# Turning the weights of mLSTM head 0 by transfers in place of TensorE, and issuing the row broadcasts of heads 1 and 2 ahead of their stores

## The chip, the cores and the metric

The kernel runs on one core of one Trainium2 chip. The metric is the device time of one execution in microseconds. The core has a matrix engine (TensorE, PE in the profile), a vector engine (VectorE, DVE), an activation engine (ScalarE, ACT), a general engine (GpSimd, POOL), a queue engine (SyncE, SP) and a set of DMA engines that move data between the core's memories and DRAM. Each engine works through its own list of instructions in order.

## The reference, cut to what matters

The model has two layers with 256 context and 256 latent tokens of width 1024. Layer 0 mixes tokens by a bidirectional mLSTM with four heads, layer 1 by latent attention; a gated convolution FFN follows each. The change touches the mLSTM alone:

```python
def step(carry, inp):                       # one chunk of one head, one direction
    ...
    b = jnp.cumsum(fc, axis=-1)
    dmat = jnp.where(tril, b[..., :, None] - b[..., None, :] + ic[..., None, :], -jnp.inf)
    ...
    wmat = jnp.exp(dmat - mj[..., None]) * jnp.einsum("bhjd,bhsd->bhjs", qc, kc)
    ...
    num = g[..., None] * jnp.einsum("bhjd,bhde->bhje", qc, C) + jnp.einsum("bhjs,bhse->bhje", wmat, vc)
    den = g * jnp.einsum("bhjd,bhd->bhj", qc, n) + jnp.sum(wmat, -1)
    h = num / jnp.maximum(jnp.abs(den), jnp.exp(-mj))[..., None]
...
hsum = o * s.transpose(0, 2, 1, 3)          # o: sigmoid output gate, s: both directions added
return _head_rms_norm(hsum, norm_g) @ w_out
```

## The kernel before

The kernel doesn't scan chunks. For each head it forms the whole 512 x 512 matrix of weights, row blocks `t` of 128 query tokens against column blocks `s` of 128 key tokens. Rows 0 and 1 (context) see columns 0 and 1; rows 2 and 3 (latent) see all four, so there are 12 blocks of 128 x 128. A block's weight is the exponential of gate sums times the scores `S`, divided by its row's normaliser and added up over the two directions. All products keep float32 accuracy by splitting an operand in a rounded high part and a low remainder (`split`: a cast on ACT, a subtraction on DVE) and multiplying three times (`mm3`, lines 447, 450 and 451).

**The stages.** `build` runs the heads in a loop. In turn h it computes the products `qk` of head h (`w_qk`: 4 outputs, each from 2 weight tiles, each tile 24 products of 128 x 512), then `av` of head h-1 (weights times values), then the scores `s_mm` of head h. Between the tiles `tick` steps background generators, two steps after each tile of `qk`. In turn 1 the generator is `head(0, S)`. In turns 2 and 3 it is `mixed(head(h-1), post)`, which steps the weights of one head and the normalisation of the head before by a plan, a string in which `h` is a step of `head`, `p` one of `post`, `L` a load that turns and `S` a split.

**The weights of a head** (`head`). Two rows of gate sums are broadcast from DRAM over 128 partitions (`aB`, line 1073, issued on POOL), masks are added (`Am`, line 1078, DVE), and three groups follow: exponentials on ACT (line 1115), products with `S` on DVE (1116), normalisers (1122 to 1126), scaling and adding of the directions (1131, 1133). The result is `P[t]`, with queries in the partitions. `av` needs keys in the partitions, so 12 turns of 128 x 128 on TensorE follow (line 1147) into three banks `PT`, each of which is split (461, 462). `av` uses `PT` as the operand that is loaded (`LDWEIGHTS`) against `v`.

**Turning by transfers** exists already for other data: `post` copies a head's output as two planes of 16-bit halves (`planes`, line 466, tile `pl`), stores the planes to DRAM (`hd`, line 1228, POOL), and `turn_load` fetches them with a transposing DMA from ACT's queue (line 1269, tile `hx`); `turn_split` splits them.

**Buffers and order.** Weight tiles `raw` are loaded by SP, cast on ACT (line 361) and reduced on DVE (384) into one of three buffers `w` (`NB`); a cast waits until PE has released the buffer. `s2` is a ring of 15 tiles of 128 x 512 that `aB`, `Am`, `W`, `S`, `pl`, `hx`, `vr` and `oh` share. `v_load` fetches the values `vr` and the output gates `oh` of a head on POOL. Beside this, background work of the modulation (`junk` and `adav`, lines 566 and 581) runs on DVE and ACT. A scheduler puts the instructions of each engine in order from the order of the code and the dependences.

Of the kernel before, what the change touches and what calls it, by code (L numbers as in the profile page):

```python
# [10 lines left out]
U16 = mybir.dt.uint16  # L11
# [23 lines left out]
NB, NRAW, NU, NS = 3, 3, 31, 15  # L35
# [381 lines left out]
class K:  # L417
# [651 lines left out]
    def head(self, h, S, big=False):  # L1069
        nc, last = self.nc, big  # L1070
        aB = [self.s2("aB0"), self.s2("aB1")]
        for d in range(2):
            nc.gpsimd.dma_start(aB[d], self.ad[d, h:h + 1, :].to_broadcast([128, 512]))
        if not big:
            self.t4_step(2)
        Am = [self.s2("Am0"), self.s2("Am1")]
        for d in range(2):
            nc.vector.tensor_tensor(Am[d].rearrange("p (t s) -> p t s", t=4),
                                    aB[d].rearrange("p (t s) -> p t s", t=4),
                                    self.mask[:, d:d + 1, :].to_broadcast([128, 4, 128]), op=ALU.add)  # L1080
        yield
        full = {0: [(0, 0), (0, 128), (0, 256), (0, 384)], 1: [(128, 256), (0, 0), (0, 256), (0, 256)]}
        P = []
        for g in range(3):
            jbs = [0, 1] if g == 0 else [g + 1]
            if big:
                w = self.uf("W")
                W = [w[:, 0:512], w[:, 512:1024]]
            else:
                W = [self.s2("W0"), self.s2("W1")]  # L1090
            den = self.tiny(4, "den")
            nd = len(jbs)
            rng = {}
            for i, t in enumerate(jbs):
                base = 256 * i if g == 0 else 0
                for d in range(2):
                    o = W[d]
                    bias = self.gcol[:, 0, t, 32 * d + h:32 * d + h + 1]
                    spans = [(t * 128, (t + 1) * 128, Am[d])]
                    if d == 0:  # L1100
                        if t > 0:
                            spans.append((0, t * 128, aB[d]))
                        lo, hi = 0, (t + 1) * 128
                    else:
                        if t == 0:
                            spans.append((128, 256, aB[d]))
                        if t >= 2:
                            spans.append((0, 256, aB[d]))
                        if t == 2:
                            spans.append((384, 512, aB[d]))  # L1110
                        lo, hi = {0: (0, 256), 1: (128, 256), 2: (0, 512), 3: (0, 512)}[t]
                    if d == 1 and t == 3:
                        nc.vector.memset(o[:, 256:384], 0.0)
                    for s0, s1, src in spans:
                        nc.scalar.activation(o[:, base + s0:base + s1], src[:, s0:s1], AF.Exp, bias=bias, scale=1.0)
                    nc.vector.scalar_tensor_tensor(o[:, base + lo:base + hi], o[:, base + lo:base + hi], 1.0,
                                                   S[g][:, base + lo:base + hi], op0=ALU.mult, op1=ALU.mult,
                                                   accum_out=den[:, 2 * i + d:2 * i + d + 1])
                    rng[i, d] = (base + lo, base + hi)
            dv = den[:, 0:2 * nd]  # L1120
            R = self.tiny(4, "R")
            nc.vector.scalar_tensor_tensor(R[:, 0:2 * nd], dv, -1.0, dv, op0=ALU.mult, op1=ALU.max)
            e = self.gcol[:, 1, jbs[0]:jbs[-1] + 1, h::32]
            nc.vector.tensor_tensor(R[:, 0:2 * nd].rearrange("p (t d) -> p t d", d=2),
                                    R[:, 0:2 * nd].rearrange("p (t d) -> p t d", d=2), e, op=ALU.max)
            nc.vector.reciprocal(R[:, 0:2 * nd], R[:, 0:2 * nd])
            for i, t in enumerate(jbs):
                big = {0: 1, 1: 0, 2: 1, 3: 0}[t]
                b0, b1 = rng[i, big]
                s0, s1 = rng[i, 1 - big]  # L1130
                nc.vector.tensor_scalar(W[big][:, b0:b1], W[big][:, b0:b1], R[:, 2 * i + big:2 * i + big + 1], None,
                                        op0=ALU.mult)
                nc.vector.scalar_tensor_tensor(W[big][:, s0:s1], W[1 - big][:, s0:s1],
                                               R[:, 2 * i + 1 - big:2 * i + 2 - big], W[big][:, s0:s1],
                                               op0=ALU.mult, op1=ALU.add)
                P.append((W[big], b0))
            yield
        for _ in range(5 if last else 1):
            yield
        self.PT = []  # L1140
        for grp in ([(t, s) for s in range(2) for t in (0, 1)], [(t, s) for s in range(2) for t in (2, 3)],
                    [(t, s) for s in (2, 3) for t in (2, 3)]):
            pt = self.ps("PT")
            lead = None
            for n, (t, s) in sorted(enumerate(grp), key=lambda x: -x[1][0] * (x[1][0] > 1)):
                src, b0 = P[t]
                q = nc.tensor.transpose(pt[:, n * 128:(n + 1) * 128], src[:, b0 + s * 128:b0 + (s + 1) * 128], self.ident)
                if lead is None:
                    lead = q
                elif t > 1:  # L1150
                    self.behind(q, [lead])
            u = self.u("PT")
            self.split(u[:, 0], u[:, 1], pt)
            self.PT.append(u)
        yield

    def v_load(self, h):
# [34 lines left out]
    def av(self, h):  # L1192
        nc = self.nc
        PT, v = self.PT, self.vh
        ts = []
        for t in range(4):
            ps = self.ps("av")
            if t < 2:
                blocks = [(PT[0], s, s) for s in range(2)]
            else:  # L1200
                blocks = [(PT[1], s, s) for s in range(2)] + [(PT[2], s, s + 2) for s in range(2)]
            for n, (u, i, s) in enumerate(blocks):
                c = slice(i * 256 + (t % 2) * 128, i * 256 + (t % 2) * 128 + 128)
                self.mm3(ps, (u[:, 0, c], u[:, 1, c]), (v[s][:, 0], v[s][:, 1]), n == 0, n == len(blocks) - 1)
            ts.append(ps)
        for t in range(4):
            nc.vector.tensor_tensor(self.oh[t], ts[t], self.oh[t], op=ALU.mult)
        r = self.oh
        self.PT = self.vh = self.oh = None
        return r  # L1210
# [36 lines left out]

    def mixed(self, head, post):

        plan = "p hp h hL h hL . L hS LS h S S . . ."  # L1250
        for step in plan.split():
            for op in step:
                if op in "hp":
                    next(head if op == "h" else post, None)
                elif op == "L":
                    self.turn_load()
                elif op == "S":
                    self.turn_split()
            yield
# [1289 lines left out]
```

## Time and profile before

| | us |
|---|---|
| median of 3 timed runs | 1339.59 (1339.39 to 1340.36) |
| the profiled execution, its own time | 1341.12 |
| its span, first to last instruction | 1339.1 |
| granted TensorE clock, mean | 0.999 |
| products `qk` of head 1, in which head 0's weights are made | 401.6 to 446.5 |
| twelve turns of head 0 | 417.9 to 421.4 |
| twelve turns of head 1, of head 2 | about 486, about 543 |

The prediction quotes rows of several views. A row of a timeline reads: start, duration, engine, line, operation, output<-inputs, partitions x elements, and in brackets the idle time before it with what ended it. A row of a group has the smallest, the median and the largest duration in ns. A row of waits names who waited, for whom, and the total, the number and the longest.

### The profile page before, as it was taken

How to read it: one execution, taken by the hardware profiler on the slowest of the kernel's cores; microseconds unless marked ns; L12 is line 12 of the kernel's file. 1: busy time of each engine (PE TensorE's matmuls, PEld its weight loads, DVE VectorE, ACT ScalarE, POOL GpSimd, SP SyncE). 2: the span in 40 equal slices, each digit the busy share in tenths (PEclk: the TensorE clock that was granted, in tenths of full speed). 3: DMA queues.
4: the chain of work that ended last, by engine and by line, in shares of the span. 5: the costliest groups of instructions: out<-in, count | busy, mean ns of one | idle time of the engine just before them, and what ended most of it. 6: DMA issues, size and time to landing. Idle time of an engine off the chain costs nothing.

```text
span 1339.1 us, 18750 instructions
## 1 busy us (share of the span) xinstructions
PE 1326.7 (99%) x6573; PEld 1111.3 (83%) x6573; DVE 1077.2 (80%) x1783; ACT 729.9 (55%) x1271; POOL 165.3 (12%) x268
## 2 busy tenths in 40 slices
PE   8999999999999999999999999999999999999997
PEld 5777888888888888888898888888888988988876
DVE  4798957678688596987979978768899889899996
ACT  4765544445734555574643334333567768567772
POOL 0212000011110111120002011111000022020100
PEclk9999999999999999999999999999999999999999
DMA  9988947889685486875628989967967597497791
GB/s 366 324 276 290 333 161 252 243 270 313 235 262 190 156 245 200 295 276 209 228 75 276 322 264 283 280 177 180 321 223 221 175 243 222 165 303 233 250 336 49
DMA packets 116990, 325.52 MB, mean 243 GB/s; under 512 B 21416, under 2 KB 40360, under 8 KB 116624
## 3 DMA queue, kind: packets, MB, share of 16 engines
q1 hardware_dynamic: 64288, 223.37, 48.6%
q0 software_dynamic: 33360, 81.43, 22.7%
q10 hardware_dynamic: 19248, 19.54, 4.5%
q8 instruction: 51, 0.84, 0.2%
q14 instruction: 43, 0.35, 0.1%
HBM read 289.51 MB, written 56.80 MB: 259 GB/s over the span
## 4 chain that ended last, share of the span: by engine, by line
PE 98%; DVE 1%; DMA 0%; issue 0%; ACT 0%; SPq 0%; DVEq 0%; ACTq 0%
PE fin L1573 8%; PE y L450 6%; PE y L451 6%; PE y L447 6%; PE tok L447 6%; PE tok L450 6%; PE tok L451 6%; PE fin L447 6%; PE fin L451 6%; PE fin L450 6%; PE qk L447 4%; PE qk L451 4%; PE qk L450 4%; PE up L746 2%; PE up L447 2%; PE up L450 1%
## 5 line engine op out<-in xcount | busy, mean ns | idle before, releaser
L361 ACT CAST w<-raw 128x1024 fp32r<-128x1024 f32 (+2 forms) x290 | 300.0, 1037 | 263.6 <-PE tok L451 74.1
L384 DVE TENSOR_TENSOR w<-raw,w 128x1024 fp32r<-128x1024 f32 (+2 forms) x290 | 347.7, 1202 | 114.5 <-ACT w L361 111.0
L566 DVE SCALAR_TENSOR_TENSOR junk<-ar,bc 128x1024 f32<-128x1024 f32 x128 | 155.8, 1218 | 5.1 <-ACT bc L608 2.2
L450 PE MATMUL fin<-h,w 128*128 128x512 f32 (+1 forms) x370 | 139.6, 377 | 0.0
L447 PE MATMUL fin<-h,w 128*128 128x512 f32 (+1 forms) x370 | 139.5, 377 | 0.0
L451 PE MATMUL fin<-h,w 128*128 128x512 f32 (+1 forms) x370 | 139.3, 377 | 0.0
L1573 PE MATMUL fin<-h,w 128*128 128x512 f32 (+1 forms) x636 | 111.1, 337 | 0.0
L1573 PEld LDWEIGHTS fin<-h,w 128*128 128x128 f32 x636 | 97.6, 190 | 13.2
L447 PE MATMUL qk<-xc,w 128*128 128x512 f32 x256 | 100.1, 391 | 0.0
L451 PE MATMUL qk<-xc,w 128*128 128x512 f32 x256 | 99.7, 389 | 0.0
L450 PE MATMUL qk<-xc,w 128*128 128x512 f32 x256 | 99.6, 389 | 0.0
L450 PEld LDWEIGHTS fin<-h,w 128*128 128x128 f32 x370 | 69.6, 188 | 13.0
L451 PEld LDWEIGHTS fin<-h,w 128*128 128x128 f32 x370 | 69.6, 188 | 12.9
L447 PEld LDWEIGHTS fin<-h,w 128*128 128x128 f32 x370 | 69.6, 188 | 12.6
L451 PEld LDWEIGHTS qk<-xc,w 128*128 128x128 f32 x256 | 48.0, 188 | 10.0
L447 PEld LDWEIGHTS qk<-xc,w 128*128 128x128 f32 x256 | 48.1, 188 | 9.9
L450 PEld LDWEIGHTS qk<-xc,w 128*128 128x128 f32 x256 | 48.1, 188 | 9.9
L384 DVE TENSOR_TENSOR wu<-raw,wu 128x1024 fp32r<-128x1024 f32 (+1 forms) x42 | 49.6, 1205 | 4.7 <-ACT wu L361 4.3
L447 PE MATMUL tok<-w,hT 128*128 128x512 f32 x128 | 49.9, 390 | 0.0
L450 PE MATMUL tok<-w,hT 128*128 128x512 f32 x128 | 49.8, 389 | 0.0
L451 PE MATMUL tok<-w,hT 128*128 128x512 f32 x128 | 49.8, 389 | 0.0
L763 ACT ACTIVATE fg<-fg 128x512 f32<-128x512 f32 (+1 forms) x44 | 23.1, 525 | 47.6 <-DVE fg L761 41.2
(520 smaller groups left out, 3146.4 us busy)
## 6 DMA issues: line engine op xcount, KB each, us to landing
raw<-in_ws SPq DMA_DIRECT2D x279, 512.0 KB, 5.3
ar<-in_adaT SPq DMA_DIRECT2D x80, 512.0 KB, 5.7
t4d<-in_ws POOLq DMA_DIRECT2D x20, 512.0 KB, 8.6
zd<-in_ws POOLq DMA_DIRECT2D x18, 512.0 KB, 11.3
adaw<-in_ada SPq DMA_DIRECT2D x16, 512.0 KB, 7.9
raw<-zd SPq DMA_DIRECT2D x12, 512.0 KB, 5.2
zr<-fd ACTq DMA_DIRECT2D x33, 128.0 KB, 4.9
xmd<-xr POOLq DMA_DIRECT2D x16, 256.0 KB, 4.6
```

Source lines behind the costliest of these rows:

```text
L361: self.cast = k.nc.scalar.copy(h[:, :cols], src)
L384: i = self.k.nc.vector.tensor_sub(l[:, :n], src, h[:, :n])
L447: q = mm(out, w[0], x[0], start=start, stop=False, skip_group_check=on)
L450: mm(out, w[0], x[1], start=False, stop=False, skip_group_check=on)
L451: mm(out, w[1], x[0], start=False, stop=stop, skip_group_check=on)
L566: nc.vector.scalar_tensor_tensor(o, w, 1.0, self.bc[j], op0=ALU.mult, op1=ALU.mult, accum_out=col[:, k, j:j + 1])
L746: nc.tensor.matmul(ps[m], wk[i][:, c], hT[k][:, j], start=made[m] == 0, stop=made[m] == 23)
L763: nc.scalar.activation(tmp[:, :n], tmp[:, :n], AF.Silu)
L1573: self.nc.tensor.matmul(ps[:, 0:256] if x else ps, w[x][:, k * 128:(k + 1) * 128], h[:, 0:256] if x else h, start=i == 0 and not k0, stop= ...
```

## The change

Three things change.

1. `head_turn` is new. For head 0 `head` hands `P` to it in place of the twelve turns on TensorE. It copies the four row blocks as 16-bit planes on ACT (three tiles `pl`: rows 0 and 1 share one), stores them by six DMAs on POOL into two DRAM tensors (`wa`: 512 rows by 256 key columns; `wb`: rows 256 to 511 by the other 256), fetches each column block by a transposing DMA from ACT's queue into `wx` (two of 128 x 1024 halves, two of 128 x 512 into one tile), and splits the three tiles `wx` into `PT`. The `yield`s in it spread this over steps 5 to 16 of the stage's sixteen.
2. `PT` becomes a table by block, so that `av` finds a block in either layout. The products of `av` are the same.
3. In heads 1 and 2 `head` yields once after its two broadcasts `aB`, and the plan of `mixed` begins with `hp hp` in place of `p hp`: the broadcasts are issued ahead of the planes and stores of `post`.

```diff
         for d in range(2):
             nc.gpsimd.dma_start(aB[d], self.ad[d, h:h + 1, :].to_broadcast([128, 512]))
+        if h and not big:
+            yield
         if not big:
             self.t4_step(2)
...
             yield
+        if h == 0:
+            yield from self.head_turn(P)
+            return
         for _ in range(5 if last else 1):
             yield
...
+    def head_turn(self, P):
+        nc = self.nc
+        da = self.dr.tile([512, 2, 256], U16, name="wa")
+        db = self.dr.tile([256, 2, 256], U16, name="wb")
+        for g, wait in enumerate((1, 3, 1)):
+            for _ in range(wait):
+                yield
+            pl = self.pool.tile([128, 2, 512], U16, tag="s2", name="pl", bufs=NS)
+            for t, c in ((0, slice(0, 256)), (1, slice(256, 512))) if g == 0 else ((g + 1, slice(0, 512)),):
+                self.planes(pl[:, :, c], P[t][0][:, c])
+            for i in range(2):
+                c = slice(i * 256, (i + 1) * 256)
+                t = i if g == 0 else g + 1
+                d = db[(g - 1) * 128:g * 128] if g and i else da[t * 128:(t + 1) * 128]
+                nc.gpsimd.dma_start(d, pl[:, :, c])
+        yield
+        xs = []
+        for s in range(4):
+            if s % 2 == 0:
+                yield
+            d, n = (da, 512) if s < 2 else (db, 256)
+            if s != 3:
+                x = self.s2("wx")
+                xs.append(x)
+            o = x[:, 256:512] if s == 3 else x[:, 0:n]
+            nc.scalar.dma_start_transpose(o.bitcast(U16), d.rearrange("t h n -> (t h) n")[:, s % 2 * 128:s % 2 * 128 + 128])
+        self.PT = {}
+        for i, x in enumerate(xs):
+            yield
+            u = self.u("PT")
+            self.split(u[:, 0], u[:, 1], x)
...
-        plan = "p hp h hL h hL . L hS LS h S S . . ."
+        plan = "hp hp h hL h hL . L hS LS h S S . . ."
```

**On PE**, in the products `qk` of head 1 (`W` are the weights of row block 2 or 3, `xc` and `w` the operands of `qk`), the second group of turns stood like this before:

```order
L450 MATMUL qk<-xc,w 128x512
L451 MATMUL qk<-xc,w 128x512
L1147 MATMUL PT<-ident,W 128x128 x2
L1147 MATMUL PT<-ident,W_3531 128x128 x2
L1147 MATMUL PT<-ident,W 128x128 x2
L1147 MATMUL PT<-ident,W_3531 128x128 x2
L447 MATMUL qk<-xc,w 128x512
```

and now nothing stands between the products:

```order
L450 MATMUL qk<-xc,w 128x512
L451 MATMUL qk<-xc,w 128x512
L447 MATMUL qk<-xc,w 128x512
L450 MATMUL qk<-xc,w 128x512
L451 MATMUL qk<-xc,w 128x512
```

The first group, four turns of rows 0 and 1 nine products earlier, is gone in the same way. Beside these twelve turns PE's order is what it was, to the end of the program.

**On ACT**, at the same place, from the cast of `w` at which the turned banks were read, before:

```order
L361 CAST w<-raw 128x1024
L461 CAST PT<-PT 128x512
L581 COPY adav<-w 1x1
L461 CAST PT<-PT 128x512 x2
L461 CAST qk<-qk 128x512
L361 CAST w<-raw 128x1024
L581 COPY adav<-w 1x1 x2
L361 CAST w<-raw 128x1024
L581 COPY adav<-w 1x1
L461 CAST qk<-qk 128x512
L461 CAST v<-vr 128x512 x4
L361 CAST w<-raw 128x1024
```

and now, from the copy of the last plane (the other copies stand ahead of it):

```order
L466 COPY pl<-W 128x1024
L461 CAST qk<-qk 128x512
L361 CAST w<-raw 128x1024
L1190 DMA_TRANSPOSE wx<-wa 128x1024 x2
L581 COPY adav<-w 1x1 x2
L361 CAST w<-raw 128x1024
L581 COPY adav<-w 1x1
L1190 DMA_TRANSPOSE wx<-wb 128x512 x2
L461 CAST qk<-qk 128x512
L461 CAST v<-vr 128x512 x4
L361 CAST w<-raw 128x1024
L461 CAST PT<-wx 128x512 x3
```

The transfers stand ahead of the next two casts of `w` and wait there for the stores; the casts of `PT` moved behind a third.

**On POOL**, whose list is its queue of DMAs, from head 0's loads to the stores of its turned output (`t4d` are loads of FFN weights), before:

```order
L1740 DMA t4d<-in_ws 16x8192 x2
L1162 DMA vr<-vd 128x512 x4
L1168 DMA oh<-od 128x512 x4
L1228 DMA hd<-pl 128x1024 x2
L1073 DMA aB_3975<-ad 128x512
L1228 DMA hd<-pl 128x1024 x2
L1073 DMA aB_3976<-ad 128x512
```

and now:

```order
L1781 DMA t4d<-in_ws 16x8192 x2
L1179 DMA wa<-pl 256x1x256 x3
L1179 DMA wb<-pl 256x1x256
L1179 DMA wa<-pl 256x1x256
L1179 DMA wb<-pl 256x1x256
L1206 DMA vr<-vd 128x512 x4
L1212 DMA oh<-od 128x512 x4
L1073 DMA aB_3969<-ad 128x512
L1073 DMA aB_3970<-ad 128x512
L1269 DMA hd<-pl 128x1024 x4
```

Six stores stand ahead of the loads of `v`, and the broadcasts of head 1 stand ahead of the stores `hd`. The same happens to the broadcasts of head 2.

More of the change, by code (lines that the diff above doesn't have):

```diff
@@ L1137, in head @@
             yield
+        if h == 0:
+            yield from self.head_turn(P)
+            return
         for _ in range(5 if last else 1):
             yield
-        self.PT = []
+        self.PT = {}
         for grp in ([(t, s) for s in range(2) for t in (0, 1)], [(t, s) for s in range(2) for t in (2, 3)],
@@ L1153, in head @@
             self.split(u[:, 0], u[:, 1], pt)
-            self.PT.append(u)
+            for n, x in enumerate(grp):
+                self.PT[x] = u, slice(n * 128, (n + 1) * 128)
+        yield
[25 more added lines that the diff above has]
+            nc.scalar.dma_start_transpose(o.bitcast(U16), d.rearrange("t h n -> (t h) n")[:, s % 2 * 128:s % 2 * 128 + 128])
+        self.PT = {}
+        for i, x in enumerate(xs):
+            yield
+            u = self.u("PT")
+            self.split(u[:, 0], u[:, 1], x)
+            for t, s in [(t, i) for t in range(4)] if i < 2 else [(t, s) for s in (2, 3) for t in (2, 3)]:
+                c = t * 128 if i < 2 else (s - 2) * 256 + (t - 2) * 128
+                self.PT[t, s] = u, slice(c, c + 128)
         yield
@@ L1197, in av @@
             ps = self.ps("av")
[L1198 to L1204, printed above, removed]
+            n = 2 if t < 2 else 4
+            for s in range(n):
+                u, c = PT[t, s]
+                self.mm3(ps, (u[:, 0, c], u[:, 1, c]), (v[s][:, 0], v[s][:, 1]), s == 0, s == n - 1)
             ts.append(ps)
```

## The prediction

> **What bounds the kernel now.** I read the busy times first, then the chain that ended last, then what TensorE waited for, then the windows around the changed place.
>
> ```profile
> PE 1326.7 (99%) x6573; PEld 1111.3 (83%) x6573; DVE 1077.2 (80%) x1783; ACT 729.9 (55%) x1271; POOL 165.3 (12%) x268
> ...
> PE 98%; DVE 1%; DMA 0%; issue 0%; ACT 0%; SPq 0%; DVEq 0%; ACTq 0%
> ```
>
> TensorE (PE) is busy for 1326.7 of 1339.1 us, and 98% of the chain that ended last is its work. Only what shortens PE's own row, or leaves PE waiting, can move the end. All that PE waits for in the execution stands in five rows (engine and line, then what it waited for: total us, times, longest):
>
> ```profile
> PE idle L683 <- DVE adav L519: 1.5, 1, 1.5
> PE adar L531 <- DMA adaw<-in_ada: 1.5, 1, 1.5
> PE y L447 <- ACT u L1797: 0.5, 1, 0.5
> PE y L450 <- DVE w L384: 0.3, 1, 0.3
> PE up L746 <- DVE hT L721: 0.3, 1, 0.3
> ```
>
> That is 4.1 us, at the start and in the last FFN product, none of it near the change. The change lies in the products `qk` of heads 1 to 3; their windows (stretch; us in it; busy us and instructions of PE, PEld, DVE, ACT, POOL; clock; DMA share; GB/s):
>
> ```profile
> 400.00:420.00 20.00, 20.00 (x93) 16.54 (x92) 18.50 (x51) 11.29 (x27) 2.68 (x5) 1.00 0.56 184
> 420.00:440.00 20.00, 20.00 (x94) 16.67 (x93) 14.72 (x27) 8.04 (x16) 0.00 (x0) 1.00 0.49 146
> 440.00:460.00 20.00, 20.00 (x96) 16.78 (x95) 13.57 (x23) 9.54 (x20) 0.00 (x0) 1.00 0.49 158
> 460.00:480.00 20.00, 20.00 (x90) 16.57 (x89) 11.66 (x35) 13.70 (x28) 6.94 (x13) 1.00 0.82 216
> 480.00:500.00 20.00, 20.00 (x96) 16.70 (x95) 19.77 (x34) 11.88 (x23) 1.60 (x3) 1.00 0.84 284
> ```
>
> PE is busy for 20.00 of 20.00 us in each, at full granted clock. The first three windows hold head 0's weights, which the change turns in another way. The last two hold head 1, where four such transfers run already for other tiles, with a DMA share of 0.82 to 0.84, and PE loses nothing.
>
> **The change, part by part.**
>
> *Removed from PE: twelve turns.* Around them PE's timeline reads (start, us, engine, line):
>
> ```profile
> 417.68 0.39 PE L451 MATMUL qk<-xc,w 128*128 128x512 f32 x1
> 417.90 0.60 PE L1147 MATMUL PT<-ident,W 128*128 128x128 f32 x4
> 418.26 0.48 PE L447 MATMUL qk<-xc,w 128*128 128x512 f32 x1
> 418.58 0.39 PE L450 MATMUL qk<-xc,w 128*128 128x512 f32 x1
> ...
> 420.19 0.39 PE L451 MATMUL qk<-xc,w 128*128 128x512 f32 x1
> 420.42 1.03 PE L1147 MATMUL PT<-ident,W 128*128 128x128 f32 x8
> 421.21 0.48 PE L447 MATMUL qk<-xc,w 128*128 128x512 f32 x1
> 421.52 0.40 PE L450 MATMUL qk<-xc,w 128*128 128x512 f32 x1
> ```
>
> Undisturbed, a `qk` product starts every 0.227 us: from 421.52 to the first product of `av` at 446.47 (row below) stand 110 of them in 24.95 us. From L451 at 417.68 to L450 at 418.58, two slots on, are 0.90 us in place of 0.45, so four turns cost 0.45. From 420.19 to 421.52 are 1.33, so eight cost 0.88. Sum **1.33 us, 0.11 each**. The chain has the same:
>
> ```profile
> 418.07 0.44 PE PT L1147 x4
> ...
> 420.58 0.87 PE PT L1147 x8
> ```
>
> That is 1.31. I take 1.32. Every other PE instruction keeps its place, so this is the whole direct gain. The turns' own duration is longer:
>
> ```profile
> L1147 PE MATMUL PT<-ident,W x48: 270/272/273, 417.9 to 591.7; 128*128 128x128 f32 x48
> ```
>
> The 272 ns overlap with the neighbours, so they bound the gain from above: 12 x 0.272 = 3.26 us. From below it is bounded by nothing gained. The page "VectorE: DVE Perf Modes" of the Trainium skill, section "The three transpose paths", gives 390 ns for a 128x128 bf16 turn on TensorE and 1309 ns for one by DMA, and its rules for kernel authors prefer TensorE where PSUM will do, which speaks against this change. By that figure the twelve would be 4.7 us (an estimate from the page) and the time 1334.9; the trace's 0.11 us of pitch decides against it.
>
> *Added: planes, stores, transfers, splits.* The rows that price them are those of head 1's turned planes (`pl`, `hd`, `hx`), in the order copy on ACT, store's issue on POOL, its landing (the issues' view from 455 to 512 us), the transfer's issue on ACT's queue, its landing, and the landings of all eight stores:
>
> ```profile
> L466 ACT COPY pl<-oh x8: 1038/1048/1052, 459.5 to 520.6; 128x1024 uint16<-128x1024 uint16 x8
> L1228 POOL DMA_DIRECT2D hd<-pl x8: 539/542/547, 460.8 to 521.9; - x8
> ...
> hd<-pl POOLq DMA_DIRECT2D x4, 256.0 KB, 3.1
> oh<-od POOLq DMA_DIRECT2D x4, 256.0 KB, 8.5
> ...
> L1269 ACTq DMA_TRANSPOSE hx<-hd x8: 1174/1208/1496, 471.7 to 534.4; - x8
> DMA to landing us min/median/max: 3.4/3.6/4.4
> ...
> DMA to landing us min/median/max: 2.3/3.1/4.2
> ```
>
> ACT gets copies of three full planes, 3 x 1.05 = 3.1 us, and four transfer issues of at most 1.2 each. It is idle for about half of the windows above, so nothing of this is on the path by itself; uncovered it would cost 3.1 us plus up to 4.8 of issue. DVE gets no new instruction: the three subtractions of `PT` move. What can reach PE is lateness, so I follow the last plane (row block t=3):
>
> ```profile
> 419.04 0.75 DVE L1133 SCALAR_TENSOR_TENSOR W<-W,R 128x512 f32<-128x512 f32 x1
> ...
> 425.39 1.05 ACT L361 CAST w<-raw 128x1024 fp32r<-128x1024 f32 x1
> ...
> 430.35 1.05 ACT L361 CAST w<-raw 128x1024 fp32r<-128x1024 f32 x1 [3.59 <-PE qk L451]
> ...
> 436.27 2.18 ACT L461 CAST v<-vr 128x512 fp32r<-128x512 f32 x4
> ...
> 437.01 2.49 DVE L462 TENSOR_TENSOR v<-vr,v 128x512 fp32r<-128x512 f32 x4
> ...
> 446.47 0.39 PE L447 MATMUL av<-v,PT 128*128 128x512 f32 x1
> ```
>
> Its weights are done at 419.8, the copy at 420.9, its two stores are issued by 422.0 and land at 425.1 (3.1 each; the stores' 512-byte pieces have no row of their own, so I bound their landing by 2.3, the shortest store, and 8.5, the slowest load in that stretch, and take 3.1 as the nearest in kind). PE-paced times after 421 come 1.32 earlier: the cast of `w` at 425.39 ends at 425.1, then two transfers are issued until 427.5 and land at 431.1. The next cast of `w` ends at 430.1, the two half transfers are out by 432.5 and land by 436.1 (436.9 at 4.4). The casts of `v` end at 437.1, one more `w` at 438.1, and three `PT` casts at 0.55 each (2.18/4) end at 439.8, all data being there. On DVE `v` ends at 438.2, `w` about 439.4, three subtractions of 0.62 (2.49/4) at 441.2. PE wants the first of them at 446.47 - 1.32 = 445.15. **3.9 us to spare**, so cost nothing.
>
> *The new wait, and what stands behind it.* A tile of `w` is cast on ACT and its remainder is taken on DVE:
>
> ```profile
> L384 DVE TENSOR_TENSOR w<-raw,w 128x1024 fp32r<-128x1024 f32 (+2 forms) x290 | 347.7, 1202 | 114.5 <-ACT w L361 111.0
> ```
>
> The transfers wait in ACT's order for the stores. Behind them stands the cast of `w` that was at 430.35, then `qk`, `v`, `w`. That cast waited for PE to release one of three `w` buffers; PE then still has two tiles of 24 x 0.227 = 5.44 us, so it wants the new one 10.9 us after 429.0, at 439.9, and it is ready at 429.0 + 1.05 + 1.2 = 431.3. The cover is 8.6 us. With 2.4 of issue behind it, the stores may land as late as about 435, 13 us after their issue, before PE waits. On POOL the loads `vr` of `v` move behind the six stores: issued by 422.0 + 4 x 0.54 = 424.2, and even at 8.5 us they land at 432.7, ahead of 436.27 - 1.32 = 434.95. The loads `oh` follow by 426.3 and are needed after `av`, past 446.
>
> *Moved: the broadcasts `aB` of heads 1 and 2 ahead of the stores `hd`.* This takes away waits of DVE:
>
> ```profile
> DVE Am L1078 <- DMA aB<-ad: 15.2, 4, 6.0
> ```
>
> At most 15.2 us in four places, 6.0 at one. PE was at 20.00 of 20.00 while DVE stood, so it is worth nothing. Two POOL issues of 0.54 us stand ahead of the stores now, and the buffers of `aB` were last read by splits done before the stores are due: 1.1 us later at worst, and head 1's transfers stand behind ACT work that begins sooner. Also nothing.
>
> **Sum.** The profiled execution's span is 1339.1, its own time 1341.12, so 2.0 lie around the span. The span becomes 1337.8 and that execution 1339.8. It was 1.5 above the median of the three timed runs (1339.59; 1339.39 to 1340.36), so against the median: 1339.59 - 1.32 = **1338.3 us**. That is 0.10%, below the 0.2% (2.7 us) that a measurement of this kernel can tell from no change.
>
> **Rivals.**
> - *Given back.* If PE, being early, waits later for something that it doesn't pace, the gain goes. For it: ACT waits for loads in the next stage (row below). Against it: PE has no wait in 400 to 1270 us at all. Time 1339.6.
>
> ```profile
> ACT wu L361 <- DMA raw<-in_ws: 4.4, 3, 2.7
> ```
>
> - *The whole duration counts.* If a turn held the array for its 272 ns, 3.26 us go: 1336.3. Against it: the pitch above, read at two places. The page "TensorE: Matmul & The Clock Gate", section "Part 4: PE-mode transpose", has about 275 ns in one kernel and says that turns don't count as activity for the clock; the granted clock of 1.00 in these windows shows nothing of that.
> - *Slower: ACT stands at the transfers.* If the stores land later than 435, the cast of `w` is late and PE stands one us for each us. To be slower by 0.2% it takes 1.32 + 2.7 = 4.0 us of standing, so landings near 439, 17 us after issue, as against 3.1 and 8.5 in the rows. Six stores, eight loads and three transfers' worth of data in the same 15 us could do it if the small pieces go badly. At 5 us of standing: 1343.3.
> - *The change doesn't do what it says.* The order of PE without the twelve rows rules this out.
>
> **Chances.** Forecast 74%, given back 12%, ACT held 8%, whole duration 6%. The range reaches from the forecast less the spread of the runs before (0.97): 1337.3, a little wider 1337.2, to "given back" with the highest run's 0.77 above its median: 1340.4. The other two cases, 14%, lie outside. Faster by over 0.2%: 6%. Within: 74 + 12 = 86%. Slower: 8%.
>
> **What would show it.** Right: twelve fewer `PT` rows on PE; PE at 20.00 of 20.00 from 400 to 480; `av` of head 0 starting near 445.15 with no wait; `wx` landed before its casts; DVE's wait for `aB` in heads 1 and 2 gone and the end unmoved by it. Wrong: a wait of PE for `w` near 440 or for `PT` at `av` (ACT held); the same `av` start but an end that isn't earlier (given back); `av` near 443 (whole duration).

## The result, and the profile after

| | before | after |
|---|---|---|
| median of 20 executions each, us | 1340.01 (1339.39 to 1340.85) | 1343.05 (1337.99 to 1348.07) |
| ratio, with its 95% interval | | 1.0019 (1.0010 to 1.0028) |
| profiled execution: its own time, span | 1341.12, 1339.1 | 1339.69, 1337.9 |

The changed kernel's executions fall in two groups: nine from 1337.99 to 1340.58, median 1339.38, and eleven from 1342.74 to 1348.07. Before, all 20 lie within 1.5 us. (The ratios here and below are taken over all executions; the quotient of the two medians is 1.0023.) The profile is of an execution of the first group and shows on PE what was forecast. The page's busy times, and the windows (columns as in the prediction):

```profile
PE 1326.7 (99%) x6561; PEld 1110.4 (83%) x6561; DVE 1076.5 (80%) x1783; ACT 732.5 (55%) x1275; POOL 169.5 (13%) x274
```

```profile
400.00:420.00 20.00, 20.00 (x90) 16.52 (x89) 18.52 (x50) 13.29 (x30) 2.82 (x4) 1.00 0.46 138
420.00:440.00 20.00, 20.00 (x90) 16.57 (x89) 11.06 (x22) 6.28 (x13) 5.70 (x10) 1.00 1.06 293
440.00:460.00 20.00, 20.00 (x96) 16.78 (x95) 15.93 (x25) 11.28 (x25) 1.07 (x2) 1.00 0.67 202
460.00:480.00 20.00, 20.00 (x90) 16.57 (x89) 13.43 (x44) 13.43 (x26) 7.19 (x13) 1.00 0.90 182
480.00:500.00 20.00, 20.00 (x96) 16.73 (x95) 19.49 (x32) 12.78 (x27) 1.61 (x3) 1.00 1.03 305
```

The first product of `av`, from PE's timeline:

```profile
444.70 0.39 PE L447 MATMUL av<-v,PT 128*128 128x512 f32 x1
```

Twelve PE instructions fewer, PE at 20.00 of 20.00, no wait at `av`. But the DMA share went from 0.49 to 1.06 in 420 to 440 and from 0.84 to 1.03 in 480 to 500. The transfers say why. The first two of `wx` on ACT's queue (smallest, median and largest issue in ns), and the landings that the trace has of `wx`, which are those of these two:

```profile
L1190 ACTq DMA_TRANSPOSE wx<-wa x2: 1334/3694/6055, 424.9 to 426.2; - x2
DMA to landing us min/median/max: 11.2/11.4/11.7
```

ACT's and DVE's timelines around them:

```profile
424.86 7.42 ACTq L1190 DMA_TRANSPOSE wx<-wa  x2
442.90 0.62 ACT L461 CAST PT<-wx 128x512 fp32r<-128x512 f32 x1 [1.01 <-DMA wx<-wb]
443.56 0.69 DVE L462 TENSOR_TENSOR PT<-wx,PT 128x512 fp32r<-128x512 f32 x1 [0.23 <-ACT PT L461]
```

And `hx` in heads 1 and 2, as `wx` above:

```profile
L1310 ACTq DMA_TRANSPOSE hx<-hd x8: 1177/1992/6300, 467.1 to 533.6; - x8
DMA to landing us min/median/max: 10.8/11.0/19.5
```

One `wx` transfer kept ACT's queue for 6.06 us in place of 1.2, and the two landed after 11.2 and 11.7 us in place of 3.6. The last split of `PT` was done at 444.25, not 441.2: 0.45 us ahead of the first product of `av`. The `hx` transfers, whose instructions the change doesn't touch, went from 1.21 to 1.99 us of issue (6.3 at most) and from 3.6 to 11.0 us of landing.

### The profile page after: what moved, and what is told of

The parts are those of the page before. It is cut to its first block, busy times and chain, and to the rows that moved or that the text cites. A ratio compares the mean times of both kernels' runs of the same rounds, so it can differ in the third digit from the quotient of the medians.

```text
span 1337.9 us, 18756 instructions
## 1 busy us (share of the span) xinstructions
PE 1326.7 (99%) x6561; PEld 1110.4 (83%) x6561; DVE 1076.5 (80%) x1783; ACT 732.5 (55%) x1275; POOL 169.5 (13%) x274
## 3 DMA queue, kind: packets, MB, share of 16 engines
q0 software_dynamic: 33648, 82.22, 22.9%
## 4 chain that ended last, share of the span: by engine, by line
PE 98%; DVE 1%; issue 0%; ACT 0%; DVEq 0%; ACTq 0%
PE fin L1614 8%; PE y L450 6%; PE y L451 6%; PE y L447 6%; PE tok L447 6%; PE tok L450 6%; PE fin L450 6%; PE tok L451 6%; PE fin L451 6%; PE fin L447 6%; PE qk L447 4%; PE qk L450 4%; PE qk L451 4%; PE up L746 2%; PE up L447 2%; PE up L450 1%
```

## The experiments

The theory that I went on to test: both halves of the change put transposing transfers, which move in many small packets (4224 for 1.05 MB between 465 and 495 us of the profile after), beside big plain loads. In head 0 (half A) the loads `vr` and `oh` stand right beside `wx`; in heads 1 and 2 (half B) the earlier `aB` lets ACT reach `hx` some 5 us sooner (467.1 in place of 471.7), where `t4d` is still being loaded. Then loads land late, and in some executions PE waits. The numbers "above 1342" count executions that took longer than 1342 us; of the kernel before, run beside these kernels, that were 2 of 87.

**The same kernel again.**

> The changed kernel again, for a second profile. Its 20 timed executions went from 1337.99 to 1348.07 us (before: 1339.39 to 1340.85), and the profiled one, at 1339.69, shows PE without a wait between 400 and 600 us. Theory A (head 0's own transfers): in a slow execution PE waits for w or PT between 430 and 450 us, because ACT stands at the issues of wx (7.4 us for two in the profiled execution, where I had 2.4). Theory B (heads 1 and 2): PE waits between 465 and 500 or between 520 and 560 us, because the transfers hx, issued 5 us earlier than before, now meet the loads t4d, vr and oh (third issue 6.3 us, where it was 1.2) and hold ACT. Both expect 1338 to 1348 again. A third, C, that the chip of the first runs was at fault, expects a spread under 2 us.

Median 1339.5, ratio 1.0004 (0.9992 to 1.0015), 3 of 12 above 1342, at 1345.1 to 1345.7; the other nine are at 1338.8 to 1340.6. So theory C falls: the two groups are the kernel's own. How many executions fall in the upper one differs, 11 of 20 above and 3 of 12 here. Its profile, of an execution at 1339.32, has no wait of PE between 395 and 700 us and so leaves A and B open.

**Half A alone**: the turn of head 0 without the moved broadcasts.

```diff
-        if h and not big:
-            yield
-        plan = "hp hp h hL h hL . L hS LS h S S . . ."
+        plan = "p hp h hL h hL . L hS LS h S S . . ."
```

> Only head 0's weights turned by transfers; the broadcasts of heads 1 and 2 where they were before. A: a spread of several us stays, median 1341 to 1344. B: the spread goes, median 1338.5 (the 1.3 us that PE is spared), all within 1.5 us.

Median 1341.29, ratio 1.0019 (1.0003 to 1.0035), 5 of 12 above 1342. The quotient of the medians is only 1.0006; one execution at 1353.81 makes up part of the ratio. The seven executions below 1342 have a median of 1340.93, which is not below the 1340.53 of the kernel before. `wx` issues took up to 6.2 us and landed after 11.6, as in the whole change; `hx` was back at 3.9.

**Half B alone**: the kernel before, with the extra `yield` and the plan `hp hp` only.

> Only the broadcasts of heads 1 and 2 moved; head 0 turned on PE as before. A: as before, 1340.0 within 1 us, since DVE's waits for aB were off the path. B: a spread of several us, median 1342 to 1345, with hx landing after 11 us as against 3.4.

Median 1343.11, ratio 1.0016 (1.0005 to 1.0026), 7 of 12 above 1342. The groups of `hx`:

```profile
L1271 ACTq DMA_TRANSPOSE hx<-hd x8: 1177/1609/7215, 465.2 to 537.7; - x8
DMA to landing us min/median/max: 5.6/12.2/18.1
```

So the moved broadcasts, which the prediction had put at nothing, bring the upper group by themselves. Another profile of this kernel fell in it:

> The kernel of e3 once more, for a profile of a slow execution (7 of its 12 were above 1342). B: if it is slow, PE waits for w between 465 and 500 or 525 and 560 us, and the granted clock is below 1.00 in the window behind the wait. If it is fast, hx lands after 8 to 18 us again with PE unheld.

It took 1343.61, and PE waited 1.4 us at `av` for the split of `v` and 1.0 at `PT`, neither of them a wait for `w` as expected, and the clock stayed at 1.00 behind them. Loads `raw` landed after up to 16.2 us (8.3 in the kernel before). DVE's row ahead of that split of `v` (`ar` is a load of background work):

```profile
502.43 1.22 DVE L566 SCALAR_TENSOR_TENSOR junk<-ar,bc 128x1024 f32<-128x1024 f32 x1 [6.30 <-DMA ar<-in_adaT]
```

**`wx` issued by SP** in place of ACT, to free ACT's queue.

```diff
-            nc.scalar.dma_start_transpose(o.bitcast(U16), ...)
+            nc.sync.dma_start_transpose(o.bitcast(U16), ...)
```

> The changed kernel with head 0's four transfers issued from SP's queue in place of ACT's, so that ACT doesn't stand at them; SP's weight loads stand behind them instead, which have about 15 us of lead (raw issued at 409.56 is cast at 425.39). A: the spread goes or shrinks to what late landings leave, median 1338.5 to 1340. B: as the changed kernel, 1338 to 1348.

A miss: median 1347.64, ratio 1.0057 (1.0036 to 1.0078), 4 of 6 above 1342. The transfers landed after 10.2 us there too, and now the loads `raw` stand behind them on SP. So freeing ACT's queue does not help; as SP's queue is held in its place, the run doesn't tell how much of the harm is the holding of a queue.

**Half A with head 0's loads ahead of the stores**, so that they are over when `wx` starts.

```diff
-VE = {1: (3, 0), 2: (3, 0), 3: (3, 0)}
+VE = {1: (1, 0), 2: (3, 0), 3: (3, 0)}
```

> Head 0 turned by transfers, broadcasts as before (as in e2), but the loads vr and oh of head 0 are traced five tiles of qk earlier, so that POOL issues them ahead of the six stores and they are through when the transfers start. Theory A1 (the transfers wx stand because 2 MB of loads run at the same time): issues of wx near 1.2 us each, landing under 6 us, ACT's idle time at them under 2 us, median 1338.5 to 1339.0, spread under 2 us. A2 (the transfers are slow whatever runs beside them): landing stays near 11 us and the spread stays, median 1341 as e2.

```profile
L1188 ACTq DMA_TRANSPOSE wx<-wa x2: 1266/1378/1489, 425.9 to 427.3; - x2
DMA to landing us min/median/max: 5.3/5.3/5.3
```

These two issues are back at 1.5 us at most (the other two took 1.9 at most), the landing at 5.3, as A1 said. Its time was a miss: median 1339.94 and not 1338.5 to 1339.0, ratio 1.0004 (0.9992 to 1.0016), and with 2 of 11 above 1342, up to 1348.44, the spread is not gone.

**Half A with more load beside `wx`**: four needless copies of 512 KB behind `oh`.

```diff
+        if h == 0:
+            more = self.dr.tile([4, 512, 2, 256], U16, name="more")
+            with self.tc.issue_after(i.ins):
+                for s in range(4):
+                    nc.gpsimd.dma_start(more[s], self.da)
```

> As e2, with four needless copies of 512 KB from DRAM to DRAM issued on POOL behind the loads oh of head 0, while wx is under way: the suspected cost doubled. A1: wx lands after 15 us or more, ACT stands over 10 us, every execution is slow, 1345 or more, and the profile shows PE waiting for w or PT between 430 and 450 us. A2: no change against e2, 1341.

All four executions are above 1346 (median 1354.16, ratio 1.0099, 1.0065 to 1.0133). From the profile of the quickest of them, the first two of `wx` with their landing, and then PE's waits:

```profile
L1188 ACTq DMA_TRANSPOSE wx<-wa x2: 1384/7326/13267, 424.5 to 425.9; - x2
DMA to landing us min/median/max: 17.4/17.7/18.0
```

```profile
PE qk L451 <- DVE w L384: 2.7, 2, 2.0
PE qk L447 <- ACT w L361: 1.5, 1, 1.5
```

Here the rival of the prediction happens: ACT stands at the transfers for 14.7 us, longer than the cover of 8.6, the cast of `w` is late and PE waits. In the changed kernel it stood 7.4, within the cover.

**Half B with `t4d` issued behind `oh`** in heads 1 and 2, out of the way of `hx`.

```diff
-        if not big:
+        if h == 0:
             self.t4_step(2)
...
+        if h:
+            with self.tc.issue_after(i.ins):
+                self.t4_step(2)
```

> As e3 (only the broadcasts moved), with the two 512 KB loads t4d of heads 1 and 2 issued behind vr and oh in place of ahead of them. B1 (hx, now issued 5 us earlier, meets t4d): hx lands after about 4 us, median 1340, spread under 2 us. B2 (it meets vr and oh): hx lands after 8 us or more, the spread stays, median 1341 to 1344.

```profile
L1274 ACTq DMA_TRANSPOSE hx<-hd x8: 1176/1258/2870, 464.9 to 532.3; - x8
DMA to landing us min/median/max: 3.8/4.6/10.8
```

Median 1339.32, ratio 0.9995 (0.9986 to 1.0004), none of 11 above 1342. Two loads per head moved out of the way take the whole loss of half B away. Not that every load is early now: in this profile `vr` of head 1 lands after up to 20.4 us and `raw` after 20.8, and PE waits for neither.

**The whole change with both mendings**, and **both mendings without the change**:

> The whole change with both orders of loads mended: head 0's vr and oh are loaded ahead of the stores of its turned planes, and the two t4d loads of heads 1 and 2 stand behind their vr and oh. Theory (small-piece transfers beside big loads): wx issues within 2.0 us, hx issues within 3 us, landings 4 to 6 us; no group of executions above 1342; median 1338.0 to 1339.4, ratio 0.998 to 0.9995, since the 1.3 us of removed turns remain. Rival 1 (the turn through DRAM itself or its waits cost something, whatever runs beside it): a second group above 1342 stays and the median is 1340 to 1343. Rival 2 (the removed turns were never worth anything): median 1339.6 to 1340.8 with no second group.

> The kernel before with those two moves of loads alone: no turn of head 0 by transfers, no broadcast moved. Theory: the loads move in spans where nothing waits for them, so ratio 0.999 to 1.001, median 1339.5 to 1340.8; then what e9 gains over this one is the 1.3 us of removed turns. Rival: the loads' places are worth 1 us by themselves (they also clear raw and hx in the kernel before), median 1338.5 to 1339.3, and then the turns are worth nothing.

The first: median 1339.29, ratio 0.9997 (0.9985 to 1.0009), 1 of 11 above 1342 (1346.73). Its median is where the theory put it, but the transfers are not: in the profile, of an execution at 1339.26, `wx` was issued in up to 4.4 us and landed after 9.5, and `hx` after up to 17.3:

```profile
L1190 ACTq DMA_TRANSPOSE wx<-wa x2: 1365/2898/4430, 425.7 to 427.2; - x2
DMA to landing us min/median/max: 9.5/9.5/9.5
```

The second is a miss for the theory as I had put it: 1343.55, ratio 1.0027 (1.0014 to 1.0039), 8 of 11 above 1342. In it `hx` lands well (4.1 us), so it doesn't take a late `hx` to lose time. With the old, later place of `hx` the loads `vr`, `oh` and now `t4d` crowd behind it: `oh` lands after 19.0 us and `t4d` after 15.6 in head 1, and the cast of `w` waits 11.6 us for `raw`. But half B with `t4d` behind `oh`, which loses nothing, has the same wait. ACT's rows of this kernel, then of that one:

```profile
492.93 1.05 ACT L361 CAST w<-raw 128x1024 fp32r<-128x1024 f32 x1 [11.64 <-DMA raw<-in_ws]
```

```profile
492.78 1.05 ACT L361 CAST w<-raw 128x1024 fp32r<-128x1024 f32 x1 [11.31 <-DMA raw<-in_ws]
```

In the first PE stands 0.7 us at 511.83, 1.5 at 539.49 and 0.5 at 545.72, in the second nowhere between 395 and 700 us. So late loads alone don't make the loss; what holds PE in the first is not shown, and neither is which of its two moved orders costs.

**Needless copies in the kernel before**, two of 512 KB in each of heads 1 and 2, right behind `t4d` and so beside `hx`; then the same copies behind the last `oh`, when `hx` has landed.

```diff
+        if h and not big:
+            with self.tc.issue_after(self.t4i.ins):
+                self.more()
```

> The kernel before, with nothing of the change, and two needless 512 KB copies from one place of HBM to another in each of heads 1 and 2, issued right behind the t4d loads, so that they run while the four hx transfers are issued (471.7 to 476.6 us in the profile of before). Theory (a transfer in small pieces beside big plain loads is issued and lands late): hx issues of 3 us and more where before had at most 1.5, landings of 8 us and more where it had 3.6, and a group of executions above 1342, median 1341 to 1345. Rival (it was the edits themselves, not what runs beside them): hx as before, median 1339.5 to 1341.

> The same copies in the same heads, issued instead behind the last oh load (486.8 us in the profile of before), when the hx transfers have landed: as many bytes and as many issues as the other kernel, beside no transfer in small pieces. Theory: hx issues at most 1.5 us, landings 4 us, every execution below 1342, median 1339.5 to 1341. Rival (it is the bytes alone that make loads late, wherever they run): the same second group above 1342 as with the copies beside hx.

Beside `hx`: median 1352.38, ratio 1.0090 (1.0077 to 1.0104), five of five above 1347. Behind it: 1340.35, ratio 0.9998 (0.9990 to 1.0007), one of 11 above 1342, where none was expected. The same bytes and the same issues cost 12 us or nothing, by where they stand. A rival stays untested: beside `hx` is also ahead of the loads `vr` and `oh` of the same head, so the copies may do their harm to these plain loads without the transposing transfers. Two expectations were off: the issues were 2.8 us at most and the middle landing 5.5, less than expected, and the cost was more. The loads `raw` landed after up to 15.1 us (8.3 before), and in the profile PE stood longest, 3.6 us, at the turns of head 3.

**Four more profiles of the changed kernel**, to have an execution of the upper group.

> The changed kernel, profiled again, for an execution of its longer group (its first two profiles were of 1339.7 and 1339.3 us). Theory (small-piece transfers beside big loads): where the time is above 1342, PE waits 1 to 4 us in all between 400 and 600 us, for a tile whose chain goes back to a late load or a late transfer (w, v, PT, qk), and the granted clock is lower there or behind it. Rival (a lower clock by itself, with nothing late): PE waits for nothing there and the clock is below 1.00 over the whole span.

> As the first of these looks: above 1342, PE waits 1 to 4 us in all between 400 and 600 us behind late loads or transfers (theory), or nothing is late and only the clock is lower (rival). Below 1341, PE waits for less than 0.5 us there by either.

> As the first of these looks: above 1342, PE waits 1 to 4 us in all between 400 and 600 us behind late loads or transfers (theory), or nothing is late and only the clock is lower (rival). Below 1341, PE waits for less than 0.5 us there by either.

> As the first of these looks: above 1342, PE waits 1 to 4 us in all between 400 and 600 us behind late loads or transfers (theory), or nothing is late and only the clock is lower (rival). Below 1341, PE waits for less than 0.5 us there by either.

They took 1356.64, 1339.49, 1344.62 and 1338.89. In the second and fourth PE waits for nothing between 400 and 600 us. The first of them, by PE's waits, by three windows, and by `hx` and `wx`:

```profile
PE av L450 <- DVE v L462: 10.5, 2, 6.0
PE PT L1152 <- ACT mod L581: 1.5, 1, 1.5
```

```profile
480.00:500.00 20.00, 20.00 (x96) 16.71 (x95) 14.81 (x23) 10.01 (x21) 1.07 (x2) 1.00 1.16 150
500.00:520.00 20.00, 15.54 (x65) 12.56 (x64) 16.50 (x25) 6.33 (x14) 0.54 (x1) 0.83 0.79 280
560.00:580.00 20.00, 13.98 (x51) 10.96 (x50) 11.42 (x17) 7.97 (x13) 1.07 (x2) 0.83 0.76 236
```

```profile
L1310 ACTq DMA_TRANSPOSE hx<-hd x8: 1177/3422/6172, 465.7 to 541.0; - x8
DMA to landing us min/median/max: 11.0/19.4/26.1
```

```profile
L1190 ACTq DMA_TRANSPOSE wx<-wa x2: 1387/3804/6220, 424.0 to 425.5; - x2
DMA to landing us min/median/max: 11.5/11.8/12.1
```

`wx` is as late as in the executions of the lower group, and PE passes head 0 without a wait; `hx` lands after up to 26.1 us, and PE stands 4.5 and 6.0 us at the `av` of heads 1 and 2. The chain to the first of these, from SP's, DVE's and PE's timelines:

```profile
484.49 3.40 SPq L589 DMA_DIRECT2D ar<-in_adaT  x2
...
503.29 1.22 DVE L566 SCALAR_TENSOR_TENSOR junk<-ar,bc 128x1024 f32<-128x1024 f32 x1 [6.78 <-DMA ar<-in_adaT]
505.05 2.49 DVE L462 TENSOR_TENSOR v<-vr,v 128x512 fp32r<-128x512 f32 x4
...
505.78 0.79 PE L450 MATMUL av<-v,PT 128*128 128x512 f32 x1 [4.46 <-DVE v L462]
```

The load `ar` that DVE needs here was issued by 487.89 (the next one only at 491.18, and that lands after 16.2 us, later than DVE goes on), so it took over 15 us to land. DVE waits 6.8 us for it, the split of `v` stands behind that in DVE's order, and PE waits for `v`. In the second profile the same instruction of DVE starts at 494.40 with no wait. The third profile has one wait of 3.8 us at head 3's `PT`, with `raw` landing after up to 18.8 us. The span of the first is 17.5 us above the mean of the second and fourth (1337.7 and 1337.1); 12.0 are these waits, where 1 to 4 were expected, and 4.9 are the lower clock behind them, by an estimate from windows of 4 us (PE's busy time from 504 to 512 and from 572 to 580, each times what its clock lacked of 1.00). The rival, a lower clock with nothing late, falls: in windows of 20 us from 400 to 620 the clock of the first and third profiles is 1.00 in all but three, and in these three PE waited.

**Two more profiles of half A alone.**

> The turn of head 0 alone, profiled again, for an execution of its longer group (5 of 12 were above 1342 us). Theory: above 1342, the wx transfers land at 11 us or later and PE's wait goes back to a load or a transfer that was late beside them, in head 0 or in what follows, 1 to 3 us in all; below 1341 PE waits for less than 1 us between 400 and 600 us. Rival (in this half as in the other it is hx that is late): above 1342, the wait stands in heads 1 to 3 behind hx transfers that land at 8 us or later.

> As the first of these two looks, with the same numbers for the theory and for the rival.

They took 1340.84 and 1346.32. In the second `wx` landed after 15.0 us, and DVE's timelines tell the rest, first of the second, then of the first (the last split of `PT`, the first mask `Am`), with the wait on PE:

```profile
447.00 0.69 DVE L462 TENSOR_TENSOR PT<-wx,PT 128x512 fp32r<-128x512 f32 x1 [1.33 <-ACT PT L461]
470.63 0.69 DVE L1078 TENSOR_TENSOR Am<-aB,mask 128x512 f32<-128x512 f32 x1 [5.91 <-DMA aB<-ad]
481.11 0.50 PE L447 MATMUL qk<-xc,w 128*128 128x512 f32 x1 [1.62 <-ACT w L361]
```

```profile
442.74 1.89 DVE L462 TENSOR_TENSOR PT<-wx,PT 128x512 fp32r<-128x512 f32 x3
466.96 0.69 DVE L1078 TENSOR_TENSOR Am<-aB,mask 128x512 f32<-128x512 f32 x1 [5.84 <-DMA aB<-ad]
```

In the second `PT` is done 3.1 us later, and everything behind it on DVE 3.6 us later, `Am` included; then the casts of `w` come late and PE waits 1.6, 1.5 and 0.6 us in head 1 and 0.3 and 0.5 in head 2, 4.5 in all where 1 to 3 were expected (0.3 and 0.5, in head 1, in the first). With the broadcasts moved, `Am` of head 1 doesn't stand behind all that: in the profile after it runs at 461.20, with no wait. So half B seems to take away the way by which half A's lateness reaches PE, and brings a loss of its own; no profile of the whole change has `wx` as late as 15.0, so the first part is argued from these rows and not shown.

## Why the prediction was wrong

The forecast was 1338.3 us, 1.3 less than before; the median went to 1343.05.

- **What bounds the kernel**: right. PE is full wherever nothing comes late.
- **Twelve turns, 1.32 us**: right on PE. From the first product of `sl` (first the row before, then after) to the first of `av` were 48.84 us before and are 47.49 now, 1.35 less:

```profile
397.63 0.40 PE L447 MATMUL sl<-qk 128*128 128x512 f32 x1
```

```profile
397.21 0.40 PE L447 MATMUL sl<-qk 128*128 128x512 f32 x1
```

  The whole duration as the gain is refuted. From the same product of `sl` to the start of the last product `y` (1272.17 before, 1270.46 now) it is still 1.29 less. That the timed runs end earlier by it is not shown: half B alone, with all its turns on PE, has a lower group of 1339.52 in the middle, and 1339.32 with `t4d` moved, against 1339.38 and 1339.31 of the whole change and 1339.29 of its mended form.
- **The turn chain, 3.9 us to spare**: its terms "at most 1.2" of issue and 3.6 of landing were taken from `hx` in the kernel before and measured 6.06 and 11.4. I took as a property of the transfer what was one of its surroundings: there `hx` was issued from 471.7 to 476.6, `t4d` at 464.7, and `vr` at 476.6. Of the 3.9 us, 0.45 were left. The sum set the last split of `PT` against the first product of `av`, and that was too strict: in the second profile of half A alone the last split ends at 447.69, 3.0 us behind the first product at 444.68, and PE doesn't wait at `av`. The lateness reached PE by a path that the sum didn't have, through DVE's order to `Am` and `w` of head 1.
- **The new wait**: the stores landed after 2.3 to 5.9 us, the last one for `wa` after 3.9 where 3.1 was taken, and PE didn't wait for `w` in head 0. ACT did stand 7.4 us at the transfers, through their issue and not through late stores. The rival's time of 1343.3 is close to the median by luck: PE never stood for this in a profile of the changed kernel.
- **Moved broadcasts, "also nothing"**: the step that failed. DVE's waits for `aB` in heads 1 and 2 went as said. I had written that "head 1's transfers stand behind ACT work that begins sooner" and took sooner for harmless; I asked what would wait for them, and not what would run beside them 5 us sooner. Half B alone, put at nothing, costs 1.0016 (1.0005 to 1.0026) with 7 of 12 executions above 1342, and moving `t4d` out of the way of `hx` takes all of it back. Half A alone has an upper group too (5 of 12), for which the turn chain's two terms are the step that failed.
- **"PE loses nothing" at a DMA share of 0.84**: one profiled execution of a kernel with 20 like executions could not show how near the edge that stage was.

None of the mended versions is measurably faster than the kernel before. In the lower group the changed kernel's median is 0.6 us below before's (1339.38 to 1340.01), and in its repeat 1.2 (1339.31 to 1340.53). As half B alone has the same lower group, the turns need not be its cause. Of the theory it is shown that the transposing transfers are issued and land later beside plain loads (`wx` after 11.6 us, 5.3 with the loads ahead of it, 17.7 with more), and that the upper group of half B goes with the place of `t4d`. What stays open: why an execution falls in one group or the other, where half B's lower group gains, and why the same move of `t4d` helps behind the moved broadcasts and not without them.

## What to carry to other kernels

When work is moved earlier, list the DMAs that it issues and what will be in flight beside them then; a transfer's duration read in one place holds only for that company. Keep transposing DMAs clear of big loads by order, or move the load that nobody waits for, and time each such move: the one of `t4d` helped half B and was part of a kernel that lost 1.0027 without it. Where slack is down to a few us, one profile is one draw: time many executions and profile again until a long one is caught.

## What the runs showed of the hardware

*The same transposing transfers can take a tenth of the DMA engines' time or all of it.* The DMA view for 484 to 492 us, of before, then of the second of the four profiles (1339.49) and of the first (1356.64) (all queues; then queue: packets, MB, share of 16 engines):

```profile
DMA packets 903, 3.19 MB, mean 399 GB/s; under 512 B 127, under 2 KB 127, under 8 KB 902
q1 hardware_dynamic: 493, 1.82, 57.9%
```

```profile
DMA packets 1436, 2.69 MB, mean 337 GB/s; under 512 B 826, under 2 KB 826, under 8 KB 1435
q1 hardware_dynamic: 560, 2.06, 74.9%
q10 hardware_dynamic: 738, 0.18, 10.2%
```

```profile
DMA packets 879, 0.76 MB, mean 95 GB/s; under 512 B 741, under 2 KB 741, under 8 KB 878
q10 hardware_dynamic: 708, 0.18, 106.4%
q1 hardware_dynamic: 71, 0.27, 9.4%
```

Before, no transposing packet (queue q10) moves in this window. In the two executions of the changed kernel q10 moves the same 0.18 MB, once in 10.2% of the engines' time beside 2.06 MB on SP's queue (q1), and once in 106.4% (times of packets are added up, and some overlap) beside 0.27. So plain loads don't crawl wherever a transposing transfer is in flight; they did where its packets took some ten times as long. Over 465 to 495 us q10's share was 22.9 to 29.1% in four profiles of the changed kernel below 1342, and 67.1% in the first of the four; in half B it was 22.4% in the execution at 1339.52 and 55.6% in the one at 1343.61. The third profile of the four, at 1344.62, has 25.1% there, but 37.2% over 520 to 560, where those four have 20.9 to 25.6. It isn't the mark of every long execution: with the copies beside `hx` the share over 465 to 495 was 24.4%. Why the packets take longer, and whether the crowd of loads is its cause or its effect, is not shown.

The Trainium skill's page "Advanced Engine Details and Errata", section "X-Bar Transpose (TRN2)", says that transposing DMAs are as fast as regular ones. Where little else ran the traces agree: in the kernel before `hx` landed after 3.4 us at the quickest, and the plain loads `oh` of head 0, also of 256 KB, after 2.8 to 4.2. Beside each other both kinds are late, in the first of the four profiles `hx` with 11.0 to 26.1 us and `vr` of head 1 with 10.9 to 14.5.

*A wait costs more than itself.* The first profile again, in windows of 4 us behind the wait that ended at 505.78 (the clock is the third number from the end):

```profile
504.00:508.00 4.00, 2.22 (x5) 1.82 (x6) 4.00 (x8) 1.71 (x3) 0.54 (x1) 0.50 0.86 344
508.00:512.00 4.00, 4.00 (x14) 3.15 (x13) 4.00 (x6) 1.33 (x3) 0.00 (x0) 0.73 0.66 199
```

After 4.5 us of standing PE ran at half its clock, and so it did after 3.65 us with the copies beside `hx` (0.50 from 596 to 600). After single waits of 1.4 to 1.5 us in three other profiles the clock stayed at 1.00, and also after two of 1.6 and 1.5, 2.3 apart, in half A. The Trainium skill's page "TensorE: Matmul & The Clock Gate", section "Part 1: The HAM clock gate", has the clock halved after an idle window of about 3.4 us, and these rows agree. The run with more load beside `wx` is less simple: two waits of 1.5 and 2.0 us with 2.7 between their ends were followed by 0.68 in 444 to 448.
